# First-stage buffers: two for each split tile of keys and queries, one instead of two for each rotation table

## The chip, the core and the metric

The kernel runs on one core of a Trainium2 chip. A core has a matrix engine (PE), a vector engine (DVE), an activation engine (ACT), a general engine (POOL) and a queue engine (SP) that here issues nearly all DMAs. Each engine works through its own instructions strictly in order; semaphores make one engine wait for another. The metric is the device time of one execution in microseconds (us); lower is better.

## What is computed

One inference step of a backbone with two layers, for 2048 sample tokens and 256 prompt tokens (2304 rows of width 1024). Each layer is

```
h = rms_norm(x) * (1 + scale) + shift
(da_q, da_k, da_v, da_g, s5_u, ..., mla_cq, mla_ckv, mla_kr, mla_g) = split(h @ w_in)
a = differential attention(rope_2d(da_q), rope_2d(da_k) + cached keys, da_v + cached values)
b = S5 scan,  c = HGRN2 recurrence,  d = latent attention(..., rope_2d(mla_kr))
x = x + gate * (concat(a, b, c, d) @ w_out)
```

`rope_2d` turns pairs of rows of the queries and keys by an angle that depends on the token's place in a 64-wide grid. All products are in float32; the kernel makes one float32 product of three passes (high part times high part, and the two cross terms), so an operand is first split into a rounded "hi" and a rest "lo".

## The kernel before

Each layer has three phases: `first_stage`, `mixers`, `out_proj`. Only the first stage is touched. It weaves two generators: `proj1`, which projects the normalised rows to the queries, the keys, the latent-attention inputs `cqk` and the values, and `s5_build`, which prepares the tables of the S5 scan on POOL, DVE, ACT and PE (`psk`, `pswz` are its PE tiles, `cp`, `tw`, `wz`, `mp`, `so` its SBUF tiles).

`proj1` goes over six blocks of 384 tokens. In each block PE computes five products `psF` (two row groups of keys, `dak`; two of queries, `daq`; one of `cqk`), 24 matmuls each, and then three products `psT` (the values), 24 matmuls each. Four PSUM banks are shared by `psF` and `psT`. `evac1` takes a `psF` away:

- ACT copies it to `x32` (L372, or L364 for `cqk`). In the last block, which holds the prompt's tokens, PE also transposes `x32` (`pso`, L338) for an output.
- DVE rotates it in `rope` (L324 shuffle, L326 times `cos`, L327 times `sin`, L328 sum `rt`).
- `split2` has ACT cast `rt` to `sphi` (L169) and DVE subtract to `splo` (L173). For `cqk` the same two buffers are called `krhi` and `krlo`.
- SP stores them to the DRAM tensors `KD`, `QD` or `KRD` (L355, L349, L350): two stores of one part and one of the other.

Every tile is taken from a pool with a tag. A tag has so many buffers, by the pool's number (2 for the pool `pj`) or by `bufs=`. A new tile of a tag waits until all readers of the tile that had the buffer before are done; for `sphi` and `splo` the readers are the store DMAs. `x32` and the rotation's two scratch tiles have one buffer each.

```
    r32 = rope(g, p, x32, (0, 128), tok0, n, "rp")
    hi = p.tile([128, 384], F32R, tag="sphi", name="sphi", bufs=1)
    lo = p.tile([128, 384], F32R, tag="splo", name="splo", bufs=1)
    split2(g, hi, lo, r32)
```

The order of the instructions on each engine is set by a list scheduler at build time, which plays the program through with modelled durations (`schedule_with_timeline_sim`); in the first half of `mixers` PE's order is as written. So a change of buffers also moves instructions.

Of the kernel before, what the change touches and what calls it, by code (L numbers as in the profile page):

```python
# [10 lines left out]
F32 = mybir.dt.float32  # L11
F32R = mybir.dt.float32r
# [153 lines left out]
def split2(g, hi, lo, src, hi_eng="act", lo_eng="vec"):  # L166
    nc = g.nc
    if hi_eng == "act":
        nc.scalar.copy(hi, src)  # L169
    else:  # L170
        (nc.vector if hi_eng == "vec" else nc.gpsimd).tensor_copy(hi, src)  # L171
    e = nc.vector if lo_eng == "vec" else nc.gpsimd
    e.tensor_tensor(lo, src, hi.bitcast(F32), ALU.subtract)  # L173
# [136 lines left out]
def rope_tables(g, p, tok0, n):  # L310
    nc = g.nc
    g.tab0 = tok0
    g.cos = p.tile([128, n], F32, tag="cos", name="cos")
    g.sin = p.tile([128, n], F32, tag="sin", name="sin")
    nc.sync.dma_start(g.cos, g.A["rcos"][:, tok0:tok0 + n])
    nc.sync.dma_start(g.sin, g.A["rsin"][:, tok0:tok0 + n])


def rope(g, p, x32, rows, tok0, n, tag):
    nc = g.nc  # L320
    a, b = rows
    c0 = tok0 - g.tab0
    sh = p.tile([128, n], F32, tag=tag + "sh", name="sh", bufs=1)
    nc.vector.stream_shuffle(sh[a:b, :n], x32[a:b, :n], [i ^ 8 for i in range(32)])  # L324
    t = p.tile([128, n], F32, tag=tag + "t", name="rt", bufs=1)
    nc.vector.tensor_tensor(t[a:b, :n], x32[a:b, :n], g.cos[a:b, c0:c0 + n], ALU.mult)  # L326
    nc.vector.tensor_tensor(sh[a:b, :n], sh[a:b, :n], g.sin[a:b, c0:c0 + n], ALU.mult)  # L327
    nc.vector.tensor_tensor(t[a:b, :n], t[a:b, :n], sh[a:b, :n], ALU.add)  # L328
    return t


def out_tr(g, p, src, rows, n, dst):
    nc = g.nc
    a, b = rows
    w = b - a
    for t in range(n // 128):
        ps = pst(g, "mm", "pso")
        nc.tensor.matmul(ps[:, :w], lhsT=src[a:b, t * 128:(t + 1) * 128], rhs=g.ident[a:b, a:b], start=True, stop=True)  # L338
        o = p.tile([128, 128], F32, tag="otr", name="otr")
        nc.scalar.copy(o[:, :w], ps[:, :w])  # L340
        nc.sync.dma_start(dst(t), o[:, :w])


def store_kr(g, p, src, tok0, n):
    nc = g.nc
    hi = p.tile([128, 384], F32R, tag="sphi", name="krhi", bufs=1)[64:96, :n]
    lo = p.tile([128, 384], F32R, tag="splo", name="krlo", bufs=1)[64:96, :n]
    split2(g, hi, lo, src)
    nc.sync.dma_start(g.KRD[0, 0:32, tok0:tok0 + n], hi.bitcast(F32))  # L349
    nc.sync.dma_start(g.KRD[1, 0:32, tok0:tok0 + n], lo.bitcast(F32))  # L350


def store_qk(g, dst, parts, idx, hi, lo, sl):
    for r, part in enumerate(parts):
        g.nc.sync.dma_start(dst[4 * idx:4 * idx + 4, r * 32:(r + 1) * 32, sl], (hi, lo)[part].bitcast(F32))  # L355


def evac1(g, l, p, kind, idx, ps, tok0, n):
    nc = g.nc
    sl = slice(tok0, tok0 + n)  # L360
    cut = min(max(LS - tok0, 0), n)
    x32 = p.tile([128, 384], F32, tag="x32", name="x32", bufs=1)
    if kind == "cqk":
        nc.scalar.copy(x32[:96], ps[:96, :n])  # L364
        r0 = FROW[(kind, idx)]
        nc.sync.dma_start(g.PF[r0:r0 + 64, sl], x32[:64])
        if cut < n:
            out_tr(g, p, x32[:, cut:], (64, 96), n - cut, lambda t: g.O["new_mla_krope"][l, t * 128:(t + 1) * 128, :])
        r32 = rope(g, p, x32, (64, 96), tok0, n, "rp")
        store_kr(g, p, r32[64:96], tok0, n)  # L370
        return
    nc.scalar.mul(x32, ps[:, :n], 32 ** -0.5 if kind == "daq" else 1.0)  # L372
    if kind == "dak" and cut < n:
        out_tr(g, p, x32[:, cut:], (0, 128), n - cut, lambda t: g.O["new_diff_k"][l, t * 128:(t + 1) * 128, idx * 128:(idx + 1) * 128])
    r32 = rope(g, p, x32, (0, 128), tok0, n, "rp")
    hi = p.tile([128, 384], F32R, tag="sphi", name="sphi", bufs=1)
    lo = p.tile([128, 384], F32R, tag="splo", name="splo", bufs=1)
    split2(g, hi, lo, r32)
    store_qk(g, g.QD if kind == "daq" else g.KD, (0, 0, 1) if kind == "daq" else (0, 1, 0), idx, hi, lo, sl)

# [25 lines left out]
def cache_keys(g, l, p):  # L406
    nc = g.nc
    for i in range(2):
        kc32 = p.tile([128, 384], F32, tag="x32", name="kc32", bufs=1)
        nc.sync.dma_start(kc32[:, :256], g.A["cdk"][l, i])  # L410
        hi = p.tile([128, 384], F32R, tag="sphi", name="sphi", bufs=1)
        lo = p.tile([128, 384], F32R, tag="splo", name="splo", bufs=1)
        split2(g, hi[:, :256], lo[:, :256], kc32[:, :256])
        store_qk(g, g.KD, (0, 1, 0), i, hi[:, :256], lo[:, :256], slice(NT, NK))
    kr32 = p.tile([128, 384], F32, tag="x32", name="kr32", bufs=1)[64:96, :256]
    nc.sync.dma_start(kr32, g.A["cmr"][l])
    store_kr(g, p, kr32, NT, 256)


def proj1(g, l):  # L420
    nc = g.nc
    N = 384
    with ExitStack() as es:
# [46 lines left out]
        keep(0)  # L470
        yield
        cache_keys(g, l, p)
        for i, tok0 in enumerate(starts):
            if 0 < i < len(starts) - 1:
                prep(i + 1)
                keep(i + 1)
            if i == 2 and l == 0:
                for rows in [g.KRD[0, 32:34]] + [g.KD[i, 96:98] for i in range(8)]:
                    nc.sync.dma_start(rows.rearrange("o (a b) -> (o a) b", b=128), g.ones[0:2 * NK // 128, :])
            hi, lo = hs.pop(i)  # L480
            rope_tables(g, p, tok0, N)
            for k, (kind, idx, cols) in enumerate(FB1):
                if i == 0 and k == H1:
                    prep(1)
                    keep(1)
                m = len(cols)
                ps = pst(g, "mm", "psF")
                for kc in range(8):
                    mm3(nc, ps[:m, :N], wf[k][0][:, kc, :m], wf[k][1][:, kc, :m], hi[:, kc, :], lo[:, kc, :], kc == 0, kc == 7)
                evac1(g, l, p, kind, idx, ps, tok0, N)  # L490
                yield
# [147 lines left out]
def mla_up(g, l, w, p, ck, cq, tok0, n):  # L639
# [18 lines left out]
    for c in range(3):  # L658
        cs = slice(c * 128, (c + 1) * 128)
        ps = pst(g, "mm", "psmq")  # L660
        nc.tensor.matmul(ps[:, :n], lhsT=w.wq[:, 0, cs], rhs=cq[:, 0, :], start=True, stop=False)
        nc.tensor.matmul(ps[:, :n], lhsT=w.wq[0:64, 1, cs], rhs=cq[0:64, 1, :], start=False, stop=True)
        hi = p.tile([128, 288], F32R, tag="uh", name="quh", bufs=2)
        lo = p.tile([128, 288], F32R, tag="ul", name="qul", bufs=2)
        sc = 96 ** -0.5
        if c < 2:
            nc.scalar.mul(hi, ps[:, :n], sc)
            nc.vector.scalar_tensor_tensor(lo, ps[:, :n], sc, hi.bitcast(F32), ALU.mult, ALU.subtract)
        else:
            rope_tables(g, p, tok0, n)  # L670
            q32 = p.tile([128, 2, 288], F32, tag="sq2", name="q32")[:, 0, :]
            nc.scalar.mul(q32, ps[:, :n], sc)
            split2(g, hi, lo, rope(g, p, q32, (0, 128), tok0, n, "rp"))
        for j, x in ((0, hi), (1, lo)):
            dst = g.MQ[j, 2 * c:2 * c + 2, 0:64, sl] if c < 2 else g.MQ[j, :, 64:96, sl]
            nc.sync.dma_start(dst, x.bitcast(F32))
        yield 1
# [1130 lines left out]
```

## Time and profile before

| | us |
|---|---|
| median of 3 runs | 5360.32 |
| the 3 runs | 5353.59 to 5371.05 |
| profiled execution, its device time | 5377.43 |
| profiled execution, first to last instruction (span) | 5375.6 |
| PE busy in the span | 4758.3 (89%) |
| DVE busy | 3834.8 (71%) |
| ACT busy | 3178.6 (59%) |
| POOL busy | 1086.8 (20%) |

The first stage of the first layer runs from the start to about 460 us, that of the second layer from about 2730 to about 3140 us. An engine's busy time does not hold the time in which it waits for a semaphore. "Granted clock" is the share of PE's full clock that it was given.

### The profile page before, as it was taken

The page shows a single profiled execution, that of the slowest core. Times are in us where ns is not written, and L with a number is a line of the kernel's source. Part 1 is how long each engine was busy: PE and PEld are TensorE (multiplying, and loading weights), DVE is VectorE, ACT ScalarE, POOL GpSimd, SP SyncE. Part 2 cuts the span into 40 slices and gives each one's busy share as a digit, 9 for nine tenths or more (in the row PEclk, how much of TensorE's full clock was granted, in tenths as well). Part 3 has the DMA queues.
Part 4 walks back from the last instruction along what each step waited for, and adds up shares of the span by engine and source line. Part 5 has one row for each costly group of instructions (what it writes and reads, how often), then busy time and mean ns, then how long its engine had stood idle before and what let it go on. Part 6 is the DMA issues. An engine that isn't in the chain of part 4 may idle for free.

```text
span 5375.6 us, 81145 instructions
## 1 busy us (share of the span) xinstructions
PE 4758.3 (89%) x27920; PEld 3462.6 (64%) x27920; DVE 3834.8 (71%) x7616; ACT 3178.6 (59%) x7516; POOL 1086.8 (20%) x1323
## 2 busy tenths in 40 slices
PE   6787999999999997889978869999999989989999
PEld 5675767677666664446767747676776666644477
DVE  7654767676668886886677547676766678879877
ACT  3224877777777773235433257786777768743354
POOL 3751222222210000000227612222222100000022
PEclk8997999999998997999989979999999989989999
DMA  6455233443332214425445452334333321241253
GB/s 216 161 171 149 88 104 95 130 116 102 91 89 72 54 51 137 117 53 165 137 166 185 154 156 87 104 99 127 116 103 92 85 72 48 54 115 51 68 159 124
DMA packets 507523, 599.37 MB, mean 111 GB/s; under 512 B 147630, under 2 KB 414806, under 8 KB 507110
## 3 DMA queue, kind: packets, MB, share of 16 engines
q1 hardware_dynamic: 506630, 592.61, 36.9%
q8 instruction: 220, 3.60, 0.3%
q14 instruction: 193, 1.58, 0.1%
q0 software_dynamic: 480, 1.57, 0.1%
HBM read 378.42 MB, written 215.18 MB: 110 GB/s over the span
## 4 chain that ended last, share of the span: by engine, by line
PE 50%; DVE 18%; DMA 13%; ACT 10%; issue 4%; POOL 3%; SPq 2%; ACTq 0%; DVEq 0%; POOLq 0%
PE psav L858 5%; PE psS L870 4%; PE psF L177 4%; PE psF L178 4%; PE psF L179 4%; PE psS L817 4%; PE psmav L950 4%; ACT junk L820 3%; PE psM L961 3%; DVE nm L818 2%; DVE a L872 2%; DMA KD<-sphi 2%; ACT pp L871 2%; PE psM L963 2%; PE psM L962 2%
## 5 line engine op out<-in xcount | busy, mean ns | idle before, releaser
L818 DVE TENSOR_REDUCE nm<-psS 128x1 f32<-128x512 f32 (+1 forms) x1312 | 790.6, 626 | 353.5 <-PE psS L817 342.3
L820 ACT ACTIVATE junk<-psS,nm 128x512 bf16<-128x512 f32 (+1 forms) x1312 | 847.6, 646 | 205.9 <-DVE nm L818 186.8
L871 ACT ACTIVATE pp<-psS 128x512 f32<-128x512 f32 (+1 forms) x1184 | 653.2, 593 | 169.7 <-PE psS L870 164.0
L177 PE MATMUL psF<-h,whi 128*128 128x288 f32 x2304 | 701.7, 305 | 29.5 <-ACT whi L169 29.5
L872 DVE SCALAR_TENSOR_TENSOR a<-pp,nlam 128x512 f32<-128x512 f32 (+1 forms) x592 | 513.8, 870 | 258.4 <-ACT pp L871 257.4
L178 PE MATMUL psF<-h,whi 128*128 128x288 f32 x2304 | 692.0, 300 | 0.0
L179 PE MATMUL psF<-h,wlo 128*128 128x288 f32 x2304 | 689.4, 299 | 1.8 <-DVE wlo L173 1.8
L964 ACT ACTIVATE me<-psM 128x512 f32<-128x512 f32 (+1 forms) x592 | 345.4, 590 | 474.8 <-PE psM L963 436.4
L817 PE MATMUL psS<-ks,qs 96*128 96x512 f32 (+1 forms) x1312 | 544.0, 425 | 52.1 <-ACT junk L820 33.4
L870 PE MATMUL psS<-qs,ks 98*128 98x512 f32 (+1 forms) x1184 | 444.6, 440 | 54.8 <-ACT junk L820 39.5
L177 PEld LDWEIGHTS psF<-h,whi 128*128 128x128 f32 x2304 | 448.3, 195 | 62.6 <-ACT whi L169 31.2
L178 PEld LDWEIGHTS psF<-h,whi 128*128 128x128 f32 x2304 | 448.5, 195 | 55.6
L171 POOL CAST whi<-w 128x1024 fp32r<-128x1024 f32 x140 | 153.2, 1095 | 1626.1 <-PE psF L178 1302.9
L927 DVE TENSOR_REDUCE mnm<-psM 128x1 f32<-128x512 f32 (+1 forms) x656 | 393.3, 623 | 79.5 <-PE psM L926 77.4
L179 PEld LDWEIGHTS psF<-h,wlo 128*128 128x128 f32 x2304 | 445.5, 193 | 3.1 <-DVE wlo L173 3.1
L870 PEld LDWEIGHTS psS<-qs,ks 98*128 98x128 f32 x1184 | 206.3, 195 | 237.6 <-ACT junk L820 135.8
L817 PEld LDWEIGHTS psS<-ks,qs 96*128 96x128 f32 x1312 | 256.4, 198 | 156.7 <-ACT junk L820 93.3
L173 POOL TENSOR_TENSOR wlo<-w,whi 128x1024 fp32r<-128x1024 f32 x140 | 349.3, 2495 | 11.2
L967 DVE TENSOR_TENSOR macc<-macc,me 128x1024 f32<-128x1024 f32 x256 | 311.5, 1217 | 39.9 <-ACT me L964 38.4
L858 PE MATMUL psav<-a,dav 128*64 128x512 f32 (+1 forms) x1184 | 311.9, 647 | 17.0 <-DVE a L872 17.0
L961 PE MATMUL psM<-qs,ks 98*128 98x512 f32 (+1 forms) x592 | 274.3, 463 | 50.3 <-ACT me L964 23.6
L1369 POOL MEMSET s5rt<- 128x2 f32 x16 | 1.6, 101 | 1532.1 <-ACT s5rt L1368 1532.1
(451 smaller groups left out, 10525.5 us busy)
## 6 DMA issues: line engine op xcount, KB each, us to landing
w<-wF SPq DMA_DIRECT2D x152, 512.0 KB
h<-HD SPq DMA_DIRECT2D x64, 576.0 KB
wmod<-w_mod SPq DMA_DIRECT2D x48, 512.0 KB
HD<-hhi SPq DMA_DIRECT2D x12, 1536.0 KB
HD<-hlo SPq DMA_DIRECT2D x12, 1536.0 KB
GX<-ev SPq DMA_DIRECT2D x128, 144.0 KB
gt<-GX SPq DMA_DIRECT2D x36, 512.0 KB
PF<-ev SPq DMA_DIRECT2D x96, 144.0 KB
```

The source lines that it names most:

```text
L177: nc.tensor.matmul(out, lhsT=w_hi, rhs=x_hi, start=start, stop=False)
L178: nc.tensor.matmul(out, lhsT=w_hi, rhs=x_lo, start=False, stop=False)
L179: nc.tensor.matmul(out, lhsT=w_lo, rhs=x_hi, start=False, stop=stop)
L817: nc.tensor.matmul(ps[:, :kn], lhsT=qs[0:96, i, t * 128:(t + 1) * 128], rhs=key_cols(ks[i], k0, kn)[0:96], start=True, stop=True)
L818: nc.vector.tensor_reduce(nm[:, i, t, ci:ci + 1], ps[:, :kn], axis=AX.X, op=ALU.max, negate=True)
L820: nc.scalar.activation(out=junk[:, :kn], in_=ps[:, :kn], func=AF.Exp, bias=nm[:, i, t, ci:ci + 1], accum_out=sm[:, i, t, ci:ci + 1])
L858: x = nc.tensor.matmul(av[hh * 64:(hh + 1) * 64, :n], lhsT=v[:, kt, hh * 64:(hh + 1) * 64], rhs=aa[:, hh, :n], start=(ki == 0), stop=(ki = ...
L870: nc.tensor.matmul(ps[:, :n], lhsT=key_cols(ks[2 * hh + m], kt * 128, 128), rhs=qs[:, 2 * hh + m, :n], start=True, stop=True)
L871: nc.scalar.activation(out=pp[:, m, :n], in_=ps[:, :n], func=AF.Exp)
L872: last = nc.vector.scalar_tensor_tensor(aa[:, hh, :n], pp[:, 1, :n], nlam, pp[:, 0, :n], ALU.mult, ALU.add)
L927: nc.vector.tensor_reduce(nm[:, i, t, ci:ci + 1], ps[:, :kn], axis=AX.X, op=ALU.max, negate=True)
L961: nc.tensor.matmul(ps[:, :n], lhsT=kh, rhs=qq[:, i, :n], start=True, stop=False)
```

## The change

The tiles `sphi`, `splo`, `krhi` and `krlo` of the first stage take the pool's two buffers instead of one. The tables `cos` and `sin` take one buffer instead of two. A tile of each kind is 384 floats on 128 partitions, so the SBUF space in the pool stays the same. The latent attention's use of `rope_tables` is in a pool with one buffer already.

```diff
 def rope_tables(g, p, tok0, n):
-    g.cos = p.tile([128, n], F32, tag="cos", name="cos")
-    g.sin = p.tile([128, n], F32, tag="sin", name="sin")
+    g.cos = p.tile([128, n], F32, tag="cos", name="cos", bufs=1)
+    g.sin = p.tile([128, n], F32, tag="sin", name="sin", bufs=1)
     nc.sync.dma_start(g.cos, g.A["rcos"][:, tok0:tok0 + n])
     nc.sync.dma_start(g.sin, g.A["rsin"][:, tok0:tok0 + n])
...
 def store_kr(g, p, src, tok0, n):
-    hi = p.tile([128, 384], F32R, tag="sphi", name="krhi", bufs=1)[64:96, :n]
-    lo = p.tile([128, 384], F32R, tag="splo", name="krlo", bufs=1)[64:96, :n]
+    hi = p.tile([128, 384], F32R, tag="sphi", name="krhi")[64:96, :n]
+    lo = p.tile([128, 384], F32R, tag="splo", name="krlo")[64:96, :n]
...
 def evac1(g, l, p, kind, idx, ps, tok0, n):
-    hi = p.tile([128, 384], F32R, tag="sphi", name="sphi", bufs=1)
-    lo = p.tile([128, 384], F32R, tag="splo", name="splo", bufs=1)
+    hi = p.tile([128, 384], F32R, tag="sphi", name="sphi")
+    lo = p.tile([128, 384], F32R, tag="splo", name="splo")
...
 def cache_keys(g, l, p):
-        hi = p.tile([128, 384], F32R, tag="sphi", name="sphi", bufs=1)
-        lo = p.tile([128, 384], F32R, tag="splo", name="splo", bufs=1)
+        hi = p.tile([128, 384], F32R, tag="sphi", name="sphi")
+        lo = p.tile([128, 384], F32R, tag="splo", name="splo")
```

Three places of the instruction order show what moves. The first is on ACT in the first layer, at the end of the fifth of the six blocks: `x32_3613` and `x32_3653` are the two groups of queries, `x32_3693` is `cqk`, `evT` are copies of the values. Before:

```order
L372 ACTIVATE x32_3613<-psF_3588 128x384
L372 ACTIVATE x32_3653<-psF_3628 128x384
L169 CAST sphi_3621<-rt_3617 128x384
L364 COPY x32_3693<-psF_3668 96x384
L499 COPY evT_3733<-psT_3708 128x512
L499 COPY evT_3761<-psT_3736 128x512
L169 CAST sphi_3661<-rt_3657 128x384
L169 CAST krhi_3702<-rt_3698 32x384
```

And in the changed kernel, from the same row on:

```order
L372 ACTIVATE x32_3613<-psF_3588 128x384
L169 CAST sphi_3621<-rt_3617 128x384
L372 ACTIVATE x32_3653<-psF_3628 128x384
L364 COPY x32_3693<-psF_3668 96x384
L169 CAST sphi_3661<-rt_3657 128x384
L499 COPY evT_3733<-psT_3708 128x512
L169 CAST krhi_3702<-rt_3698 32x384
L499 COPY evT_3761<-psT_3736 128x512
```

The casts move up by one place each; the copies of the values that stood ahead of the second cast now stand behind it.

The second is on SP's queue in the first layer, ahead of the first block. `cos_1596` and `sin_1597` are the second block's tables, `wt32` weights, `xt` rows of the input. Before, the tables stand with the first loads:

```order
L355 DMA KD_75<-sphi_667 4x32x256
L410 DMA kc32_674<-cdk 128x256
L315 DMA cos_1596<-rcos 128x384
L316 DMA sin_1597<-rsin 128x384
L468 DMA wt32_523<-wT 128x1024
L280 DMA xt_1497<-x_s 128x1024
```

In the changed kernel they stand at the end of the first block, where before the third block's tables (`cos_2326`) stood:

```order
L366 DMA PF_69<-x32_1230 64x384
L355 DMA QD_76<-sphi_1170 4x32x384 x2
L355 DMA QD_76<-splo_1171 4x32x384
L500 DMA VT_78<-evT_1310 128x512
L1304 DMA SC0_65<-so_1186 128x512
L315 DMA cos_1596<-rcos 128x384
L316 DMA sin_1597<-rsin 128x384
L349 DMA KRD_72<-krhi_1239 32x384
```

Each pair of tables is thus issued about one block later than before, right after the last rotation of the block that reads the buffer.

The third is on SP at the end of the fifth block in the changed kernel. `cos_3792` and `sin_3793` are the last block's tables, `QD_76<-sphi_3661` the store of the fifth block's second group of queries; before, these tables stood one block earlier and neither row was here:

```order
L521 DMA h2_4148<-HD_77 128x4x288
L366 DMA PF_69<-x32_3693 64x384
L316 DMA sin_3793<-rsin 128x384
L355 DMA QD_76<-sphi_3661 4x32x384 x2
L355 DMA QD_76<-splo_3662 4x32x384
L315 DMA cos_3792<-rcos 128x384
L500 DMA VT_78<-evT_3733 128x512
L349 DMA KRD_72<-krhi_3702 32x384
```

The load of `sin_3793` waits for the last read of the old `sin` (L327 on `cqk`), and the query stores behind it wait with it, as they did before for the table of another block.

## Rows read from the trace of the kernel before

**Rows 1.** Stretches: length; PE, PEld, DVE, ACT, POOL busy; clock; DMA share; GB/s.

```profile
100.00:373.00 273.00, 209.67 (x1039) 184.29 (x1040) 163.55 (x363) 70.43 (x160) 191.24 (x427) 0.90 0.45 145
373.00:460.00 87.00, 66.34 (x311) 58.50 (x309) 23.44 (x52) 13.00 (x32) 3.49 (x5) 0.88 0.49 150
2800.00:3080.00 280.00, 225.06 (x1134) 195.50 (x1133) 178.20 (x442) 77.39 (x174) 198.27 (x434) 0.91 0.53 169
3080.00:3140.00 60.00, 34.21 (x159) 29.51 (x157) 11.21 (x26) 7.99 (x19) 1.69 (x3) 0.77 0.46 142
```

**Rows 2.** Waits, first layer, 100 to 460: us in total, times, longest.

```profile
ACT sphi L169 <- DMA KD<-sphi: 71.8, 11, 10.7
ACT krhi L169 <- DMA QD<-sphi: 44.8, 6, 8.4
...
ACT sphi L169 <- DMA QD<-sphi: 34.9, 6, 11.8
...
PE psk L1307 <- DVE cp L254: 29.7, 7, 12.4
...
PE pswz L1302 <- ACT mp L1308: 17.2, 7, 4.8
...
PE pso L338 <- ACT x L364: 10.6, 1, 10.6
...
PE pso L338 <- ACT x L372: 9.2, 1, 9.2
```

**Rows 3.** Waits, second layer, 2770 to 3140.

```profile
PE pso L338 <- ACT x L364: 23.1, 1, 23.1
...
PE psk L1307 <- DVE cp L254: 20.5, 9, 4.6
...
PE pst L299 <- ACT t L304: 9.7, 3, 6.1
...
PE psk L1307 <- DVE cp L257: 8.2, 5, 4.6
```

**Rows 4.** Chain that ended last within 270 to 300: start, us, what.

```profile
283.05 7.82 DMA QD<-splo
...
290.96 0.55 DVE krlo L173
```

**Rows 5.** PE in order of time; in brackets its idle time before.

```profile
292.87 1.14 PE L1307 MATMUL psk<-cp,brep 128*128 128x240 f32 x2 [12.42 <-DVE cp L254]
```

**Rows 6.** ACT's casts in order of time, last block, first layer.

```profile
415.97 0.51 ACT L169 CAST sphi<-rt 128x384 fp32r<-128x384 f32 x1 [3.24 <-DVE rt L328]
...
426.39 0.51 ACT L169 CAST sphi<-rt 128x384 fp32r<-128x384 f32 x1 [9.18 <-DMA KD<-sphi]
...
436.75 0.51 ACT L169 CAST sphi<-rt 128x384 fp32r<-128x384 f32 x1 [9.13 <-DMA KD<-sphi]
...
444.05 0.51 ACT L169 CAST sphi<-rt 128x384 fp32r<-128x384 f32 x1 [6.40 <-DMA QD<-sphi]
...
451.38 0.51 ACT L169 CAST krhi<-rt 32x384 fp32r<-32x384 f32 x1 [6.44 <-DMA QD<-sphi]
```

**Rows 7.** DVE, the sum that ends the rotation of the second tile.

```profile
418.76 0.56 DVE L328 TENSOR_TENSOR rt<-rt,sh 128x384 f32<-128x384 f32 x1
```

**Rows 8.** ACT's casts, last block, second layer (first, second and last).

```profile
3080.42 0.51 ACT L169 CAST sphi<-rt 128x384 fp32r<-128x384 f32 x1 [2.21 <-issue]
...
3103.18 0.51 ACT L169 CAST sphi<-rt 128x384 fp32r<-128x384 f32 x1 [21.53 <-DMA KD<-sphi]
...
3128.34 0.51 ACT L169 CAST krhi<-rt 32x384 fp32r<-32x384 f32 x1 [6.43 <-DMA QD<-sphi]
```

**Rows 9.** Chain, 2730 to 2742: the load of a table.

```profile
2737.59 3.20 DMA cos<-rcos
```

**Rows 10.** PE, the value products: first and last of 46 matmuls in a row.

```profile
384.81 0.39 PE L179 MATMUL psT<-wth,hlo 128*128 128x512 f32 x1
...
395.01 0.39 PE L179 MATMUL psT<-wth,hlo 128*128 128x512 f32 x1
```

## Prediction

> **What bounds the kernel now.** I read the page first: PE is busy 89% of the span, but that is an average, so I went to the two first stages. The view of busy time by stretch says that no engine is full there [rows 1]: in the first layer's loop (100 to 373 us) PE works 209.67 of 273 us, POOL 191.24, DVE 163.55, and at the end (373 to 460) PE works 66.34 of 87. The second layer reads alike. The DMA engines are about half busy (0.45 to 0.53). A stage in which nothing is full is bound by waits, so the next view was the list of waits [rows 2]: ACT stands 71.8 + 44.8 + 34.9 = 151.5 us before casts to `sphi` or `krhi`, each time for a store that still reads the one buffer. The reader is to see there that the waiting engine is not the one that is short: ACT and DVE run in order, and what is stuck behind the cast is other work. The chain around 290 us shows it [rows 4]: a query store lands after 7.82 us, DVE can then write `krlo` at 290.96, and only behind that it makes the S5 tile `cp`, for which PE has been idle for 12.42 us when it goes on at 292.87 [rows 5]. That is how the buffer reaches PE: `psk` waits for `cp`, `pswz` for `mp` on ACT, `pso` for `x32` on ACT [rows 2].
>
> **The second split buffer, in the loop.** PE's waits of this kind are 29.7 + 17.2 = 46.9 us in the first layer [rows 2] and 20.5 + 9.7 + 8.2 = 38.4 in the second [rows 3], 85.3 together; the most that the loop can give back through them. How much of it goes: one buffer makes the distance from cast to cast as long as cast, issue and landing, 444.05 - 436.75 = 7.3 us for a query, 426.39 - 415.97 = 10.4 for a key tile of the last block [rows 6]. With two buffers a cast needs the stores of the cast before the last, so two casts fit into that time: 3.65 to 5.2 us each. The compute chain itself allows a distance of about 3.4: the cast at 415.97 was followed by a finished `rt` at 418.76 + 0.56 = 419.3 [rows 6, 7]. What stays of each wait is 0.2 to 1.8 us, of 3.9 to 7.0 before, so 75 to 95% of the casts' waiting goes. PE will not get all of that, since `cp` and `mp` also hang on POOL, which is busy 70% of the loop [rows 1], and some waits of these kinds stand behind no cast. I take 70% of 85.3, 60 us. Bounds: none, if POOL's tables are late next and take the time over, and all of PE's idle time in the two loops, (273 - 209.67) + (280 - 225.06) = 118 us.
>
> **The same in the last block.** Here no S5 work is left and the five casts follow one another: 415.97 to 451.38, 35.4 us [rows 6]. With two buffers, counted from the first cast: second after 3.4, third when the first's stores are in, 10.4, fourth 3.4 + 10.4 = 13.8, fifth one query distance after the third, 10.4 + 7.3 = 17.7. That is 17.7 us less. In the second layer the second cast stands 22.8 us behind the first (3103.18 - 3080.42) because SP has other transfers in front of the key's second store, and the five take 47.9 [rows 8]. With two buffers the second cast leaves that wait, but the third inherits it: 22.8, and the fifth 22.8 + 7.3 = 30.1, so 17.8 less. PE is idle before `pso` by 10.6 + 9.2 in the first layer and 23.1 in the second [rows 2, 3], 42.9 in all, so 35.5 can indeed be passed on: the value products, the key loads and the mixers stand behind it. Bounds 0 and 42.9.
>
> The price of a store is where a rule and a row part. The row is 7.3 us from cast to cast for a query [rows 6]. The Trainium skill ("DMA: Bandwidth & Descriptors", Anatomy of one DMA) gives about 2.0 us plus the bytes at 436 GB/s, fitted on another issuing path; for 196,608 bytes that is an estimate of 2.45 us. With it the casts would stand some 4 us apart even with one buffer, next to the chain's 3.4, and the sum of 95 would shrink to about 0.6 / 3.9 of it, 15. The trace does not agree, and I go by the row.
>
> **The table's lost buffer.** No instruction is added; the ten reloads (five in each layer) are issued about one block later, after the last rotation of the block before. One load takes 3.20 us on a quiet queue [rows 9]; the trace has no table load that was waited for behind other transfers, so the upper bound is the slowest key tile of the last blocks, 22.8 from cast to cast with SP's other transfers in front [rows 8]. The cover is the three value products that PE does between two blocks, 72 matmuls at (395.01 - 384.81) / 45 = 0.227 us [rows 10], 16.3 us: a load that starts when PE is in step with the casts is hidden wholly. The place without cover is the last block, where PE has run ahead and the first key product waits in PSUM for its rotation. There I count one load per layer, nearer to the quiet price as the order puts only two or three stores ahead of it: 2 x 3.2 = 6.4 us lost; bounds 0 and 10 x 22.8 = 228.
>
> SP's waits move no further: a table load waited for a block's last rotation before, too, only for another buffer, so nothing new is queued behind it.
>
> **The rest.** The scheduler also reorders the recurrences in the mixers. These moves are swaps of neighbours with the same work, and I give them nothing, with 10 us either way for the range. The granted clock is 0.90 and 0.91 in the loops and 0.77 at the second layer's end [rows 1]; fewer pauses may lift it, but no row prices that, and it stays out of the sum.
>
> **The sum.** 60 + 35.5 - 6.4 = 89 us. The profiled execution took 5377.43, so its like would take 5288. That execution lay 17 us above the median of the runs shown, 5360.32; taken from the median, the forecast is 5271, 1.7% less. A measurement of this kernel can tell about 0.3%, 16 us.
>
> **Rivals.**
> 1. *Only the ends gain.* POOL and the S5 chain take the loop over: POOL's 191.24 of 273 us with its own waits for DVE is the fullest after PE [rows 1]. Against it: PE's longest pause there follows a store, not POOL [rows 4, 5]. Then 35.5 - 6.4 = 29 us, 5331.
> 2. *The stage comes to run at PE's pace.* All of PE's idle time in the four stretches goes, 63 + 21 + 55 + 26 = 165 us [rows 1]; for it speaks that casts 3.65 us apart keep up with `psF`. Against it: the weave with S5 and the key loads at the end. Then 5195.
> 3. *The stores only land later.* If two sets in flight share the same transfer rate, the distance per cast stays 7.3 and nothing changes, 5360. Against it: DMA is half idle [rows 1].
> 4. *Slower: the tables take the place of the stores.* The first rotation of every block then waits for its tables, DVE holds `cp` behind it, and PE pauses as it did for the stores. It decides from 95.5 / 10 = 9.6 us per load on; halfway between the two store distances seen, 10.4 and 22.8 [rows 6, 8], a load costs 16.6, and 166 - 95.5 = 70 us are lost: 5431. Against it: the 16.3 us of cover in front of each block's first rotation [rows 10]. By the Trainium skill ("Trainium Kernel Development and Optimization", Best Practices) transfers should be double-buffered so that they overlap with computing; the change takes that from the tables, and by this rule alone the reloads would be exposed. The trace before has two buffers, so it cannot show it.
>
> **How the numbers follow.** Forecast 0.55 (its own range 5235 to 5310), rival 1 0.18, rival 2 0.12, rival 3 0.08, rival 4 0.07. The range 5205 to 5340 takes in the forecast, rival 1 and the nearer part of rival 2. Faster by over 0.3%: the forecast, rivals 1 and 2, 0.85; within 0.3%: rival 3, 0.08; slower: rival 4, 0.07.
>
> **What would show it.** Right: in the list of waits, ACT's casts waiting for stores fall from 151.5 us to under 50 in the first layer; the five casts of the last block take about 18 and 30 us; `psk` and `pswz` waits fall by more than half; the DVE product with `cos` (L326) shows no wait for a table load outside the last block. The first stages end about 50 and 40 us earlier in their own time. Wrong: if L326 waits for `cos` in every block (rival 4), if casts still stand 7 us apart (rival 3), or if PE's pauses stay and name POOL (rival 1). It would also be wrong if the mixers or the output projection took 20 us or more longer after the reordering.

## The result and the profile after

The changed kernel takes 5296.23 us (median of 4 runs, 5292.0 to 5297.03) against 5359.34 us of the kernel before in the same comparison (4 runs): ratio 0.9878, 95% interval 0.9863 to 0.9893. That is 65 us less by the ratio (57 to 73); 89 had been forecast. The profiled execution took 5296.69 us, with a span of 5294.9.

The waits of the first layer's first stage, 100 to 460 us, answer to [rows 2] (us in total, times, longest):

```profile
ACT sphi L169 <- DMA KD<-sphi: 45.1, 6, 12.3
...
ACT evT L499 <- DMA VT<-evT: 29.2, 4, 10.1
...
ACT krhi L169 <- DMA QD<-sphi: 21.0, 5, 7.5
...
PE pswz L1302 <- POOL wz L257: 18.0, 6, 7.5
```

Two things are to be seen. ACT's casts wait 45.1 + 21.0 = 66.1 us for stores in place of 151.5; the 34.9 of the casts to `sphi` behind query stores are gone. And a row stands here that the kernel before did not show among its waits: ACT waits 29.2 us to copy values to `evT`, because `evT` has two buffers too and the third copy of a block needs the first one's store to have landed.

The second layer, 2770 to 3140 us, answers to [rows 3]:

```profile
ACT sphi L169 <- DMA KD<-sphi: 25.2, 4, 9.5
...
ACT evT L499 <- DMA VT<-evT: 19.6, 3, 11.6
...
ACT otr L340 <- DMA new_diff_k<-otr: 12.0, 1, 12.0
...
PE psk L1307 <- DVE cp L254: 11.2, 5, 4.7
...
PE psk L1307 <- DVE cp L257: 5.8, 4, 4.8
```

Here `otr`, the transposed keys of the last block, is another tile of two buffers that now makes ACT wait. The casts of the last block, first layer, answer to [rows 6]:

```profile
402.73 0.51 ACT L169 CAST sphi<-rt 128x384 fp32r<-128x384 f32 x1 [2.18 <-DVE rt L328]
...
411.46 0.48 ACT L340 COPY otr<-pso 128x128 f32<-128x128 f32 x2 [4.83 <-DMA new_diff_k<-otr]
...
420.35 0.52 ACT L169 CAST sphi<-rt 128x384 fp32r<-128x384 f32 x1 [4.95 <-DMA KD<-sphi]
424.26 0.51 ACT L169 CAST krhi<-rt 32x384 fp32r<-32x384 f32 x1 [3.02 <-DMA QD<-sphi]
```

The five take 424.26 - 402.73 = 21.5 us, where they took 35.4. In the second layer, to [rows 8], first cast, the wait for `otr`, last cast:

```profile
3039.65 0.52 ACT L169 CAST sphi<-rt 128x384 fp32r<-128x384 f32 x1 [2.15 <-DVE rt L328]
...
3055.54 0.48 ACT L340 COPY otr<-pso 128x128 f32<-128x128 f32 x2 [11.98 <-DMA new_diff_k<-otr]
...
3067.91 0.51 ACT L169 CAST krhi<-rt 32x384 fp32r<-32x384 f32 x1 [3.02 <-DMA QD<-sphi]
```

They take 28.3 us in place of 47.9. The loop is best measured from the first cast of the first block to the first cast of the last block. Busy time in that stretch of the first layer (columns as in [rows 1]), the kernel before, then the changed one:

```profile
114.18:415.97 301.79, 235.25 (x1175) 207.67 (x1174) 168.25 (x369) 73.44 (x166) 180.94 (x393) 0.91 0.49 157
```

```profile
111.76:402.73 290.97, 236.01 (x1175) 208.96 (x1174) 171.58 (x371) 74.24 (x167) 184.47 (x400) 0.90 0.50 165
```

PE makes the same products (1175 records) and is idle for 55.0 us in place of 66.5. The loop became 10.8 us shorter, where 70% of this layer's 46.9 would be 33. What PE waited for in this stretch before were the 29.7, 17.2 and 9.2 us of [rows 2], and then

```profile
PE pswz L1302 <- POOL wz L257: 6.5, 4, 3.2
```

After the change:

```profile
PE pswz L1302 <- POOL wz L257: 16.3, 5, 7.5
PE pswz L1302 <- ACT mp L1308: 11.8, 3, 6.2
PE pso L338 <- ACT x L372: 9.1, 1, 9.1
PE psk L1307 <- DVE cp L254: 5.3, 2, 4.3
```

The reader is to compare the sums, not the rows. The two waits that the prediction priced fell from 46.9 to 17.1 us. But `pswz`, one of the same S5 products, now waits 16.3 us for `wz` from POOL, 9.8 more than before, and smaller new waits joined. The 9.1 us before `pso` stand at the end of the loop in both kernels, 9.2 before. Before, ACT came to the copy `x` late because of its casts; now the third copy to `evT` stands ahead of it in ACT's order and waits for a store, and PE waits with it (ACT, then PE):

```profile
399.57 0.59 ACT L499 COPY evT<-psT 128x512 f32<-128x512 f32 x1 [10.13 <-DMA VT<-evT]
400.05 0.50 ACT L372 ACTIVATE x<-psF 128x384 f32<-128x384 f32 x1
```

```profile
400.60 1.23 PE L338 MATMUL pso<-ident,x 128*128 128x128 f32 x4 [9.13 <-ACT x L372]
```

### The profile page after: what moved, and what is told of

Same layout as the page of the kernel before. It is cut to its first block, busy times and chain, and to the rows that moved or that the text cites. A ratio compares the mean times of both kernels' runs of the same rounds, so it can differ in the third digit from the quotient of the medians.

```text
span 5294.9 us, 81097 instructions
## 1 busy us (share of the span) xinstructions
PE 4724.9 (89%) x27920; PEld 3434.4 (65%) x27920; DVE 3835.7 (72%) x7616; ACT 3183.3 (60%) x7516; POOL 1089.4 (21%) x1323
## 4 chain that ended last, share of the span: by engine, by line
PE 49%; DVE 18%; DMA 13%; ACT 10%; issue 4%; POOL 4%; SPq 1%; ACTq 0%; DVEq 0%; POOLq 0%
PE psav L858 5%; PE psS L870 4%; PE psF L177 4%; PE psF L178 4%; PE psF L179 4%; PE psS L817 4%; PE psmav L950 3%; ACT junk L820 3%; PE psM L961 2%; DVE nm L818 2%; DVE a L872 2%; DVE mnm L927 2%; ACT pp L871 2%; PE psM L926 2%; PE pshg L1018 2%
## 5 line engine op out<-in xcount | busy, mean ns | idle before, releaser
L870 PE MATMUL psS<-qs,ks 98*128 98x512 f32 (+1 forms) x1184 | 440.6, 436 | 53.9 <-ACT junk L820 38.7
L177 PEld LDWEIGHTS psF<-h,whi 128*128 128x128 f32 x2304 | 444.7, 193 | 65.3 <-ACT whi L169 34.5
L870 PEld LDWEIGHTS psS<-qs,ks 98*128 98x128 f32 x1184 | 203.3, 192 | 236.3 <-ACT junk L820 136.4
L173 POOL TENSOR_TENSOR wlo<-w,whi 128x1024 fp32r<-128x1024 f32 x140 | 350.3, 2502 | 11.2
L950 PE MATMUL psmav<-me,mv 128*64 128x512 f32 (+1 forms) x1184 | 318.0, 631 | 13.7 <-ACT me L964 7.9
```

The costliest lines, as they stand in the source:

```text
L177: nc.tensor.matmul(out, lhsT=w_hi, rhs=x_hi, start=start, stop=False)
L870: nc.tensor.matmul(ps[:, :n], lhsT=key_cols(ks[2 * hh + m], kt * 128, 128), rhs=qs[:, 2 * hh + m, :n], start=True, stop=True)
L950: x = nc.tensor.matmul(av[i * 64:(i + 1) * 64, :n], lhsT=v[:, kts[ki], i * 64:(i + 1) * 64], rhs=e[:, i, :n], start=(ki == 0), stop=(ki == ...
```

## Experiments

Each kernel was built anew, so the scheduler set its order anew; that holds for every difference below. Spare SBUF came from the staging slots of the weights (tag `w32`, two buffers of 4 KB), which are idle once the weights are split. Besides the ratio to the kernel before (the repeat is a single execution and has none) I read two marks from each profile. Stage 1 is the time to the first product of L870 (`psS<-qs,ks`, a line that the extra lines of some kernels shift), which stands in the mixers' first work; stage 2 runs from the last store of `X` in the first layer to the same product of the second. The rest is the span less both.

| kernel | ratio (95%) | stage 1 | stage 2 | sum | rest |
|---|---|---|---|---|---|
| before | 1 | 551.8 | 502.6 | 1054.4 | 4321.2 |
| before again | | 558.1 | 502.9 | 1061.0 | 4293.6 |
| changed | 0.9878 (0.9863 to 0.9893) | 530.7 | 473.4 | 1004.1 | 4290.8 |
| 1 only tables | 0.9992 (0.998 to 1.0004) | 560.6 | 506.4 | 1067.0 | 4281.5 |
| 2 split, two tables | 0.9884 (0.9864 to 0.9903) | 524.9 | 479.6 | 1004.5 | 4300.4 |
| 3 third `evT` | 0.9847 (0.9826 to 0.9867) | 524.8 | 466.5 | 991.3 | 4290.9 |
| 5 last block only | 0.9946 (0.9934 to 0.9958) | 543.1 | 490.9 | 1034.0 | 4303.3 |
| 6 loop only | 0.9957 (0.994 to 0.9974) | 542.5 | 490.2 | 1032.7 | 4324.6 |
| 7 light POOL | 0.992 (0.9905 to 0.9934) | 528.3 | 475.6 | 1003.9 | 4325.5 |
| 8 `HD` on POOL's queue | 0.9937 (0.9923 to 0.995) | 527.4 | 505.8 | 1033.2 | 4299.6 |
| 9 `evT` and `otr` | 0.9863 (0.9839 to 0.9887) | 517.6 | 471.5 | 989.1 | 4291.2 |
| 10 third split buffer | 0.9868 (0.9848 to 0.9889) | 514.0 | 476.4 | 990.4 | 4297.5 |
| 11 stores by ACT | 0.9832 (0.9809 to 0.9854) | 503.7 | 472.8 | 976.5 | 4285.7 |
| 12 S5 products free | 0.9911 (0.9894 to 0.9927) | 529.7 | 474.3 | 1004.0 | 4293.2 |

### The kernel before, again (no edit)

> The kernel before, unchanged, once more. In the two profiled executions the second layer's latent attention took 816.6 us before (last psS 4223.1 to last psM of L926 5039.8) and 800.2 after. If that was the one execution, this stretch comes out 5 us or more off 816.6, towards 800; if the reordering of the mixers did it, the stretch reads 816 again, within 3 us, and the changed kernel owes 16 us to the reordering.

The stretch reads 5018.6 - 4211.2 = 807.4 us: 9 less than in the first profile, 7 more than after the change. The rest of the program differs by 27.6 us between two executions of one kernel, so the first profile of before was a long one in stages that the change does not touch, and the changed kernel owes nothing there that could be told from this. The granted clock goes with it: of the fourteen profiles three have a rest above 4320 us, before, 6 and 7, and these are the three whose stretch from 4300 to 4990 us was granted 0.92; in the others it was 0.93 to 0.95, with a rest of 4281.5 to 4303.3. What sets the clock there, no run shows. The repeat is the better partner: its two stages are 56.9 us longer than those of the changed kernel, of 59.7 in the span. Its casts in the last block, first and last:

```profile
417.61 0.51 ACT L169 CAST sphi<-rt 128x384 fp32r<-128x384 f32 x1 [3.18 <-DVE rt L328]
...
452.96 0.51 ACT L169 CAST krhi<-rt 32x384 fp32r<-32x384 f32 x1 [6.44 <-DMA QD<-sphi]
```

The first cast came 14.9 us earlier after the change and the five took 13.8 us less. In the second layer, counted from the last store of `X`, 351.9 became 336.5 (15.5 earlier) and the five casts, 46.4, became 28.3 (18.1 less). From the fifth cast to the mark 1.3 and 4.1 us were given back. So the loop, with what stands ahead of it, brought 30.4 us, the ends 31.9 less 5.4, and 56.9 is the sum.

### 1 and 2. The tables apart

Run 1 takes one line of the change to the kernel before (and its twin for `sin`), run 2 gives the changed kernel two table buffers, in `proj1`:

```diff
-    g.cos = p.tile([128, n], F32, tag="cos", name="cos")
+    g.cos = p.tile([128, n], F32, tag="cos", name="cos", bufs=1)
```

```diff
-            rope_tables(g, p, tok0, N)
+            g.tab0 = tok0
+            tb = pws.tile([128, 2, 512], F32, tag="w32", name="tab")
+            g.cos, g.sin = tb[:, 0, :N], tb[:, 1, :N]
+            nc.sync.dma_start(g.cos, g.A["rcos"][:, tok0:tok0 + N])
+            nc.sync.dma_start(g.sin, g.A["rsin"][:, tok0:tok0 + N])
```

> The kernel before with one buffer for each rotation table and the split tiles still single. Theory (the tables are covered by the value products): within 0.3% of before, 5345 to 5375 us, and L326 names no table load in the loops. Rival (the lost table buffer eats part of the gain, 34 us or more over ten loads): 5385 us or more, with waits of L326 for the load of cos.

> The changed kernel with the tables in two buffers again (they lie in the idle staging slots of the weights, so the SBUF size is kept). Theory (tables cost at most the 6.4 us of the prediction): 5285 to 5302 us, no more than 0.2% from the changed kernel's 5296. Rival (the lost table buffer is where the loop's missing 34 us went): 5262 to 5275 us.

The theory held in both. One table buffer alone changes the time by -11 to +2 us (0.998 to 1.0004). The rotations (L326, L327) of that run waited for a table twice, 0.3 and 0.6 us, both in the second layer; those of the changed kernel never did. The stages of the one profiled execution are 6 to 13 us longer, but the timed runs don't bear this out. The second run gives the same total as the changed kernel; its stages trade 5.8 us for 6.2, because the staging slots come free later than the pool's own tile would in the second layer (the first table is issued there at 2754.27 us, in the changed kernel at 2704.91).

By the Trainium skill ("Trainium Kernel Development and Optimization", Best Practices) transfers should be double-buffered; taken as a rule, the tables' reloads would be exposed. These two runs and the changed kernel do not bear that out. A reload of the tables is hidden here as long as it is issued early enough for what waits behind it; runs 3 and 9 each show one that was not.

### 3. A third buffer for evT

```diff
-                o = p.tile([128, 512], F32, tag="ev", name="evT")
+                if t < 2:
+                    o = p.tile([128, 512], F32, tag="ev", name="evT")
+                else:
+                    o = pws.tile([128, 2, 512], F32, tag="w32", name="evT")[:, 0, :]
```

> The changed kernel with a third buffer for the value copies evT (the third of each block lies in the idle staging slots of the weights). Theory (the wait moved on to the next short tile in ACT's order: 29.2 us of evT waits for VT stores in the first layer's stage, 19.6 in the second's): these waits fall to under 5 us and half of them reaches PE, 5265 to 5282 us. Rival (the loop now runs at the pace of POOL's S5 chain): the waits fall as well but the waits for wz, mp and so grow by as much, 5288 to 5300 us.

As the theory said: the median is 5279.98 us, and 0.9847 against 0.9878 is about 17 us (3 to 30, estimated from the two intervals, which just overlap). The loops are 1.9 and 5.1 us shorter than in the changed kernel. No wait of `evT` for a store is left in the lists; in the second layer ACT waits for PE there, and the next short tile is longer than before:

```profile
ACT otr L340 <- DMA new_diff_k<-otr: 17.5, 1, 17.5
ACT evT L502 <- PE psT L179: 16.3, 8, 5.4
```

In the first layer the waits for KD stores went up again, from 45.1 to 54.0. And in its last block the lost table buffer now shows. The copy `x` is done at 391.96 us, but the rotation waits for `cos`, which was issued at 389.08:

```profile
398.26 0.56 DVE L326 TENSOR_TENSOR rt<-x,cos 128x384 f32<-128x384 f32 x1 [5.65 <-DMA cos<-rcos]
```

In the changed kernel `cos` was issued about as late, at 389.73, but the copy `x` began only at 400.05, so the wait of `evT` hid the load. A kernel with a third `evT` and two buffers for each table was not run; it would tell what the reload costs once `evT` is out of the way.

### 5 and 6. The last block alone, the loop alone

Both start from the kernel before. Run 5 has this helper, by which `evac1` and `store_kr` take their split tiles; run 6 has the same with `tok0 < NT - 384`.

```diff
+def split_tiles(g, p, nm, tok0):
+    if tok0 == NT - 384:
+        sp = g.spare.tile([128, 2, 512], F32R, tag="w32", name=nm + "sp")
+        return sp[:, 0, :384], sp[:, 1, :384]
+    return [p.tile([128, 384], F32R, tag="sp" + x, name=nm + x, bufs=1) for x in ("hi", "lo")]
```

> The kernel before, tables in two buffers; only the five split pairs of the last block have two buffers (in the idle staging slots of the weights), those of the five blocks before and of the cached keys have one as before. The prediction's term for the last blocks is 35.5 us: 5324 us. Theory after the first comparison (33.5 us less between the first and the fifth cast of the two last blocks): 5320 to 5335 us. Rival (a shorter last block is not passed on, because the key loads or the mixers' own work come last): 5345 us or more.

> The kernel before, tables in two buffers; the split pairs of the first five blocks have two buffers (in the idle staging slots of the weights), those of the last block and of the cached keys one. The prediction's term for the loop is 60 us: 5300 us. Theory after the first comparison (the first cast of the last block comes 13.2 and 12.6 us earlier): 26 us, 5325 to 5343 us. If the two terms simply add, the gains of this run and of the last-block run together are the 63 us of the changed kernel.

The last block alone gives 0.54% (0.42 to 0.66), 29 us (23 to 35); the loop alone 0.43% (0.26 to 0.60), 23 us (14 to 32). By the marks they bring 20 to 27 and 22 to 28, depending on which profile of before is taken. The kernel before read 5366.32 us in this comparison, so the ratio is what compares; by it both lie inside the theory's ranges. The sum, 0.97%, falls short of 1.22% by no more than the intervals allow. The prediction's 60 for the loop is excluded, its 35.5 for the last blocks just.

### 7. Less work for POOL

```diff
-        cmul(E, wz[0], wz[1], pwb[0], pwb[1], bbb[0], bbb[1], tw[:, :8, :])
+        E.tensor_tensor(wz[0], pwb[0], bbb[0], ALU.mult)
+        E.tensor_tensor(wz[1], pwb[1], bbb[1], ALU.mult)
...
-        E.tensor_tensor(tw8, pqb[1], ccb[1], ALU.mult)
-        E.tensor_tensor(car, car, tw8, ALU.subtract)
```

> The changed kernel with half of POOL's work for the S5 tables left out: wz takes one product in place of a complex one (4 of 6 operations fewer), and the first part of so two operations fewer; the tables hold other values, all else is computed on them. Theory (after the change the loop still waits for stores, of VT and KD): 5283 to 5300 us, the waits for wz shrink but those for stores grow. Rival (the loop has come to the pace of POOL's chain, the prediction's first rival in the loop): 5255 to 5275 us and the first cast of the last block 10 us or more earlier in each layer.

The first stages did not move: 1003.9 us against 1004.1. The loop of the first layer takes 400.11 - 108.05 = 292.1 us, with POOL busy 145.72 us in it in place of 184.47, a fifth less. No wait of PE for `wz` is left in it, so POOL is not what sets its pace. PE's waits, 100 to 400 us, only have other names:

```profile
PE pst L299 <- ACT t L304: 21.8, 3, 12.3
PE pswz L1301 <- ACT so L1302: 11.4, 3, 6.3
```

The total was outside both expectations, 5322.71 us. That is not the stage: the rest of the program took 4325.5 us, with a granted clock of 0.96, 0.94 and 0.92 in three stretches of the second layer's mixers (3300 to 3800, 3800 to 4300, 4300 to 4990) where the changed kernel had 0.98, 0.95 and 0.94. Between the two executions of the kernel before the last of these differs as much (0.92 and 0.94). Whether the other values, the order or chance lowered the clock here stays open; the last run, which also changes the values, has a long total too, but its profiled execution was the shortest of its six (5299.01 us) and does not show it.

### 8. The HD stores on POOL's queue

```diff
-                nc.sync.dma_start(g.HD[part, :, :, starts[i]:starts[i] + N], x.bitcast(F32))
+                nc.gpsimd.dma_start(g.HD[part, :, :, starts[i]:starts[i] + N], x.bitcast(F32))
```

> The changed kernel with the two 1.5 MB stores of each block's normalised rows (HD) issued from POOL in place of SP. Theory (the fourth cast of a block waits 6 to 12 us for key stores that are queued behind these 1.5 MB): ACT's waits for KD stores fall from 45.1 to under 20 us in the first layer, 5280 to 5292 us. Rival (the transfer engines are shared, so the key stores land as late from any queue): these waits stay over 35 us, 5292 to 5305 us, or more if the issue holds POOL up.

The mechanism held and the time did not follow. ACT's waits of `sphi` for KD stores fell from 45.1 to 7.5 us in the first layer, while those of `krhi` for QD stores rose from 21.0 to 34.5, and the loop took 392.10 - 98.99 = 293.1 us, as long as with them. PE waits 32.4 us for `cp` in it, 5.3 in the changed kernel's. Stage 2 is 32.4 us longer than in the changed kernel and as long as before. There PE waits for `cp` again (2747 to 3057 us):

```profile
PE psk L1307 <- DVE cp L254: 34.5, 12, 7.0
PE pswz L1302 <- POOL wz L254: 11.0, 5, 4.3
```

Whether POOL's issues (0.87 us each) or the new order put `cp` late is not settled.

### 9 and 10. More buffers

Both have the third `evT` of run 3 and the tables of run 2, which take turns in the two staging slots, so the tables have one buffer. Run 9 adds the first pair of lines (`ob=4` for the stage's calls), run 10 the same with `ob=3` and the second pair, with its like for `splo`, `krhi` and `krlo`:

```diff
-        o = p.tile([128, 128], F32, tag="otr", name="otr")
+        o = p.tile([128, 128], F32, tag="otr", name="otr", bufs=ob)
...
-    hi = p.tile([128, 384], F32R, tag="sphi", name="sphi")
+    hi = p.tile([128, 384], F32R, tag="sphi", name="sphi", bufs=3)
```

> The changed kernel with a third place for evT (as in the run with the third evT; the tables share these staging slots and so still have one buffer) and four buffers for the transposed keys otr of the last block, in place of two. In the run with the third evT alone ACT stood 17.46 us before an otr copy for its store in the second layer's last block (11.98 in the changed kernel, 4.83 in the first layer). Theory (the next short tile takes the wait over each time): these go, the five casts of the second layer's last block take 20 us or less in place of 33.7, and the time falls to 0.981 to 0.984 of before. Rival (what follows the last block is late for another reason): the casts come closer, but the time stays at the 0.9847 of the third evT.

> As the run with a third evT, and a third buffer for the split tiles, with the tables in the staging slots (one buffer) and three buffers for otr. The fourth cast of a block waits 6 to 18 us for key stores that stand in SP's queue behind the 1.5 MB stores of HD. Theory (this wait is what is left of the loop's gain): ACT's waits for KD stores fall from 54.0 to under 20 us in the first layer and the time to 0.978 to 0.982 of before. Rival (the loop's pace is now set by the compute chain, POOL or PE's own products): the waits fall too, but the first cast of the last block comes no more than 3 us earlier in each layer and the time is 0.982 to 0.985.

Run 9 removed the `otr` wait, and the second layer's five casts take 23.5 us (3030.36 to 3053.85) in place of 33.7 (20 had been expected; the third and fourth still wait for KD stores), but the total is not better than run 3's. It does not decide between the two expectations, because the tables' new place cost something that I had not priced. They are issued at 2732.80 in the second layer, behind the last weights, where the changed kernel issues them at 2704.91 with the stage's first loads (the run, then the changed kernel; SP, start and length of an issue):

```profile
2732.80 0.33 SPq L484 DMA_DIRECT2D tab<-rcos  x1
```

```profile
2704.91 0.46 SPq L315 DMA_DIRECT2D cos<-rcos  x1
```

Its first rotation came at 2739.31, and the first cast of the first block stands 60.9 us behind the last store of `X` (2742.48 - 2681.6), in the changed kernel 48.6. The rotations waited for the tables 6.7 us in the first layer's last block, as in run 3, and 0.8 in the second layer: this is the exposed reload that the prediction feared, here by a late issue.

Run 10 is clear on the first layer. With three split buffers no cast to `sphi` waits for a store in the first layer; only `krhi` does, 21.3 us. The loop takes 394.49 - 101.87 = 292.6 us all the same, with PE busy 235.29. PE's waits there:

```profile
PE pswz L1309 <- POOL wz L257: 20.3, 8, 8.6
PE psk L1314 <- DVE cp L254: 18.7, 7, 11.9
PE pso L338 <- ACT x L372: 8.2, 1, 8.2
```

The 8.2 us are again at the loop's end, where ACT makes `x` 15.2 us late, now behind a store of `x32`, which has one buffer. They do not hide a gain: up to this wait the loop has taken 391.33 - 8.16 - 101.87 = 281.3 us, in the changed kernel 400.60 - 9.13 - 111.76 = 279.7. The rival's view, that the loop is no longer set by the stores of the split tiles, is right. The total, 0.9868, lies above both ranges; the second layer's loop takes 296.2 us (2742.06 to 3038.23), 8.4 more than in the changed kernel, and ahead of its last block the rotation waits 8.5 us for the tables in their new place.

### 11. ACT issues the stores of the split tiles

On top of run 3, in `store_qk` and in the same way in `store_kr`:

```diff
-        g.nc.sync.dma_start(dst[4 * idx:4 * idx + 4, r * 32:(r + 1) * 32, sl], (hi, lo)[part].bitcast(F32))
+        g.nc.scalar.dma_start(dst[4 * idx:4 * idx + 4, r * 32:(r + 1) * 32, sl], (hi, lo)[part].bitcast(F32))
```

> As the run with a third evT, with the stores of the split tiles (KD, QD, KRD) issued by ACT in place of SP, so that they are not queued behind the HD stores. Theory (queue order on SP delays the stores): KD waits fall from 54.0 to under 15 us in the first layer, 0.979 to 0.983 of before. Rival (the twelve to fourteen issues of a block, some 0.35 us each, and the wait for splo hold ACT up by more than that): 0.986 or more.

The best kernel of the study, 0.9832, just outside the theory's range and below the rival's; its interval overlaps that of run 3. ACT's casts to `sphi` wait 1.5 us for KD stores in the first layer (run 3: 54.0). Most of it comes where neither theory put it: the second cast of the cached keys stands at 77.06 us (run 3: 88.27) and the first block's first at 94.09 (run 3: 110.89), probably because their stores no longer queue behind the first HD stores (in run 8, which moves the HD stores, they stand at 77.19 and 98.99), and the loop after it takes 284.2 us (run 3: 289.1). In the second layer it lost 6.3 us to run 3. There the rival may have a part, though no run shows how much: PE stands before `pswz` for `mp` on ACT,

```profile
PE pswz L1305 <- ACT mp L1311: 22.1, 4, 10.5
```

and ACT makes `mp` behind its issues, which in the whole run take 0.5 us as a rule and 5.1 at the longest.

### 12. S5 products that wait for no S5 tile

```diff
-            nc.tensor.transpose(ps_[:, 0:128], wz[i].rearrange("p s c -> p c s").rearrange("p c s -> p (c s)"), g.ident)
+            nc.tensor.transpose(ps_[:, 0:128], g.ident, g.ident)
...
-            nc.tensor.matmul(psk[:, :240], lhsT=br_[i].rearrange("p s c -> p c s").rearrange("p c s -> p (c s)"), rhs=cp[i].rearrange("p t h -> p (t h)"), start=(i == 0), stop=(i == 1))
+            nc.tensor.matmul(psk[:, :240], lhsT=g.ident, rhs=c_[i].rearrange("p a b -> p (a b)")[:, :240], start=(i == 0), stop=(i == 1))
```

> The changed kernel; PE's products for the S5 tables (the transposes pswz and the products psk) read tables that never change in place of wz, cp and brep, so PE makes the same products but waits for none of POOL's and DVE's S5 tiles; POOL and DVE still make those tiles; the S5 tables hold other values. In the changed kernel's loop of the first layer PE waits 26.5 us in front of these products for wz and cp (16.3 + 2.8 + 5.3 + 2.1), in the second 32 (11.2 + 9.2 + 5.8 + 5.8). Theory (the loop's gain was lost to these waits: with the stores out of the way, the S5 tiles themselves come too late for the place their products have in PE's order): the loop takes 15 to 25 us less in each layer, from 291.0 and 287.8 us between the first casts of the first and the last block to 275 or less. Rival (PE's idle time moves on once more, to x, t or the banks of PSUM, as it did with lighter POOL work): 284 us or more in each layer. The total is not judged, since with other S5 values the run with lighter POOL work differed in later stages as well.

My theory fell. The loops take 400.50 - 115.18 = 285.3 and 3017.51 - 2732.78 = 284.7 us, 5.7 and 3.1 less, not 15 to 25. PE and ACT in the first layer's loop:

```profile
PE psk L1307 <- ACT so L1303: 30.5, 9, 6.9
```

```profile
ACT so L1303 <- DMA SC<-so: 43.2, 11, 9.0
```

PE's idle time moved on to the next tile of two buffers, `so`, whose copies wait for its stores to `SC`. This wait of `so` for `SC` does not occur on ACT in the first layer of the kernel before or of the changed one; it shows once the others are gone.

## Why the prediction came out as it did

- **The mechanism was right.** ACT's casts waited for stores, and in order behind them stood the work that PE needs. The second buffer cut these waits from 151.5 to 66.1 us (under 50 was said). Runs 5 and 6 show that both places, the loop and the last blocks, gain by it. What is left is the wait for key stores (45.1) and for `krhi` (21.0), not that of the first queries.
- **The loop was mis-sized.** The step that failed is "I take 70% of 85.3, 60 us". The part of it on the waits was near: in the two loops the costed waits fell from 46.9 to 17.1 and from 38.4 to 17.2 (11.2 + 5.8 + 0.2), 51.0 of 85.3, 60%. But PE's idle time fell only from 66.5 to 55.0 and from 58.6 (301.28 - 242.66, 2779.14 to 3080.42) to 46.1 (287.82 - 241.69, 2751.83 to 3039.65), 24.0 us; other waits in front of the same products took the rest. The loop alone, timed in run 6, gave 23 us (14 to 32), the marks 22 to 28, the first casts 30.4.
- **Where the missing half went.** Part of it into the next short tile on ACT: the third `evT` gave about 17 us back, 13 of them in the marks and 7 in the loops, and PE's 9.1 us before `pso` show how such a wait reaches it. For the rest no single taker was found. Lighter POOL work, key stores that land in time, a third split buffer and S5 products without S5 inputs left the first layer's loop at 292.1, 293.1, 292.6 and 285.3 us. PE is busy 234 to 243 us in it and idle for 50 to 57 in all four, whatever its waits are called. That the order fixed at build time is what remains would fit, but no run changed only that; it is argued, not shown.
- **The last blocks were near.** 17.7 and 30.1 us were predicted for the five casts, 21.5 and 28.3 were measured; the first layer's is longer by the wait for `otr` (4.83), which I had not seen. That the second layer's comes near is in part luck: the third cast is held by `otr`'s store (11.98) and not, as I had it, by the key's. And one reading was wrong: of the 42.9 us before `pso`, the 9.2 stand ahead of the first of the five casts, so these cannot give them back. After the change 9.1 us are still there, by `evT`; the other two waits fell from 33.7 to 8.4 us, by 25.3. Of the 31.9 us that the casts gave in both layers 26.5 reached the mark, and the run with the last block alone gives 29 (23 to 35) against 35.5.
- **The tables cost nothing** that the measurement can show (-11 to +2 us), where 6.4 had been counted. No rotation of the changed kernel waits for one. But in the last block, where I had counted the cover as gone, it is gone: the wait of `evT` hides the load there, and without it (run 3) the rotation waits 5.65 us. That the term came out at nothing is luck in this place.
- **The order of the mixers** gave no 20 us: the rest of the program takes 4290.8 us in the changed kernel and 4293.6 in the repeat, at nearly the same granted clock (0.935 and 0.934 over the span).
- **What was to show it.** `psk` waits fell by more than half in the first layer, `pswz` waits grew. The first stages end 21 to 27 and 29 us earlier in their own time, not 50 and 40. The sign given for the first rival, pauses that name POOL, was seen in part; that POOL is the cause is refuted by runs 7 and 12.

Counted by the runs' own sizes the sum would have read 24 + 26.5 + 0 = 50.5 us from PE's idle time, or 23 + 29 = 52 from the two part runs; the change gave 57 to 73. A part of the difference may be the granted clock, which the prediction had left out of the sum. Of the 50 executions of the kernel before that stand beside the runs above, the 10 that were granted 0.934 or more took 5353.7 us in the mean, the 14 at 0.930 or less 5369.8, all 50 together 5361.6; the four of the changed kernel had 0.934 to 0.936. By that some 8 of the 65 us go with the clock, an estimate from these means; no run sets the clock by itself.

## What to carry over

A buffer that removes a wait is worth what the next short buffer behind it leaves: before pricing the waits of one tile, list every tile of one or two buffers that is emptied by a store on the same engine, and when its store lands. Waiting time that goes from an engine in order is not yet time off the path; compare the bound engine's idle time as a sum over releasers. A load with one buffer is hidden as long as it can be issued early, so ask when its slot comes free, and which wait hides it now: when that wait is removed, the load may show.

## What the runs showed of the hardware

In the changed kernel issues on SP took longer shortly behind large stores. Two stores of 1.5 MB are issued at 164.68 and 167.42 us; the issues behind them (start, length):

```profile
167.42 0.55 SPq L440 DMA_DIRECT2D HD<-hlo  x1
168.07 2.95 SPq L1336 DMA_DIRECT2D ED<-Eb  x1
...
174.01 2.00 SPq L355 DMA_DIRECT2D KD<-splo  x1
...
191.16 0.56 SPq L355 DMA_DIRECT2D QD<-splo  x1
```

A split tile's store took 2.00 us to issue there and 0.56 later. The Trainium skill says that the queues of SP, ACT and POOL run on the same transfer engines and that issuing from several saves only issue time ("Trainium Kernel Development and Optimization", Key Constraints), and also that each transfer engine takes turns between the queues it has work for, packet by packet ("DMA: Bandwidth & Descriptors", Queues, rings and completion order). The eighth run fits either: with the large stores on another queue the waits of `sphi` for key stores fell from 45.1 to 7.5 us. How much of this is SP's issue time and how much the order in the queue, no run here separates.

The two profiled executions of one kernel differ by 27.6 us outside the changed stage, nearly half of the gain that was to be explained. A difference of two single profiles has to be read stage by stage, with the same kernel profiled twice.
